# Split activations that begin two columns later: 320-column matmul operands on 16 bytes

## The chip, the cores and the metric

The kernel runs on one core of a Trainium2 chip. The metric is the device time of one execution in microseconds (us); runs before and after are compared by their medians. Single executions are given by the span between the first and last instruction that the profiler saw, and by the time of the whole execution, which is a little longer.

## The reference, cut to what matters

A trunk of two layers over 640 tokens (128 context tokens, 512 latent tokens) of width 2048. Each layer normalizes and modulates its input, multiplies it with a wide input projection, runs two mixers and a gate on parts of the result, and multiplies with an output projection:

```python
shift, scale, gate = modulation(c, ada_w[l], ada_b[l])
h = rms_norm(x, norm_g[l]) * (1.0 + scale[:, None]) + shift[:, None]
...
y, _ = even_mixer(h, w_in_even[e], ...)   # h @ w_in, attention, gated linear attention, gate
...
x = x + gate[:, None] * (y @ w_out[l])
```

Nearly all arithmetic is in `h @ w_in` and `y @ w_out`. The two shifts (one for context, one for latent tokens) are added after the projection: the kernel multiplies them with the same weights as two more columns.

## The kernel before, in words

**Layout.** Activations are stored transposed: a tile has 128 partitions (one block of 128 features) and the tokens lie along the row. There are 16 feature blocks, k = 0 to 15. fp32 accuracy comes from splitting: an activation x becomes `h` (x rounded to the format that TensorE multiplies fast, fp32r) and `l` (x − h), a weight becomes `whi` and `wlo`. One product of a 128x128 weight block and a piece of activations is three matmuls: whi·h, whi·l, wlo·h (`mm_k`, `three`).

**The four tiles.** `acth` and `actl` (`self.ah`, `self.al`, lines 275 and 276) hold the split activations, 16 rows per partition of 2 + 640 words each: two columns for the shifts, then 640 tokens. So a row has 642 words or 2,568 bytes, and the next row begins 8 bytes off a multiple of 16. `eh` and `el` (line 2418 on) hold split combinations of activations for a Strassen-like scheme (`spair`), 6 × 3 rows of `CW` = 2 + 320 words (1,288 bytes). In the compiled program each of the four tiles begins on a multiple of 16 bytes.

**The halves.** A matmul takes at most 512 columns, so the tokens are taken in two halves. `cols` (line 748) gives the columns of each: half 0 is columns 0 to 322 for a projection that needs the shifts (322 wide) and 2 to 322 for one that does not (320 wide); half 1 is columns 322 to 642 (320 wide). In the last pair (`hpair`) the cut is at 384 tokens, so its operands are 384 and 256 wide.

**Who issues matmuls.** `units`, for one output chunk of 128 features: for each four k, half 0 of the four, then half 1 of the four, three matmuls each. `kpair`, for two chunks at the ends of a projection: k by k, both halves at once, the second chunk two steps behind the first. `spair`, for two chunks by seven products instead of eight: `product` runs over the six rows of one combination, `plain` over four k that take no part in it (`JT` and `MT` name the k that are combined).

**Who writes the rows.** `act_mod` (line 1258 on) at the start; `handover` between projections: `rewrite` splits a new activation (ScalarE writes `h`, VectorE or GpSimd writes `l`), `fold` makes the rows of `eh` and `el` and rewrites half 1 of some rows of `acth` and `actl`, after saving them to DRAM (the DMA to `bh_dram` and `bl_dram`). `shifts` and `shift1` write the two shift columns.

**The rest.** `sums` is a work buffer of 322 words. The arena is one region cut by hand into slots of 640 words; its last part, `rest`, holds the slot R, and also the buffers for squares of the outputs (`sqs`, two of 320 words in turn, and `sq`, 384 words for the last pair), which are summed for the norm. All instructions are in an order that a planner in Python (`Pace`) writes out by hand: it keeps a time for each engine and for each block of 32 words of a tile, and its choices (which task to advance, which bank to take) follow from these times.

Of the kernel before, what the change touches and what calls it, by code (L numbers as in the profile page):

```python
# [9 lines left out]
F32 = mybir.dt.float32  # L10
F32R = mybir.dt.float32r
# [3 lines left out]
ALU = mybir.AluOpType  # L15
# [4 lines left out]
KT = D // 128  # L20
NCTX = 128
NLAT = 512
T = NCTX + NLAT
HT = T // 2
# [9 lines left out]
NS = len(JT)  # L34
SUB = NS // 2
NY = 8
CW = 2 + HT
RING = 2560

OUT0 = (0, 12, 1, 13, 2, 14, 3, 15, 8, 10, 9, 11, 4, 5, 6, 7)  # L40
# [200 lines left out]
class Trunk:  # L241
# [9 lines left out]
    def __init__(self, tc, d, es):  # L251
        self.tc, self.d, self.es = tc, d, es
        self.pace = Pace()
        self.nc = Core(self.pace, tc.nc)
        self.n = 0
        self.now = 0.0
        self.turn = {}
        self.tasks = []
        self.low = None
        self.stall = 0.0  # L260
        self.flags = set()
        self.actset = None
        self.folded = self.quiet = False
        self.cut = HT
        self.room = self.rooms[0]
        nc = self.nc
        self.per = es.enter_context(tc.tile_pool(name="per", bufs=1))
        self.sml = es.enter_context(tc.tile_pool(name="sml", bufs=6))
        self.wraws = self.P([128, 2048], "wraw")
        self.whl = [self.P([128, RING], n, F32R) for n in ("whi", "wlo")]  # L270
        ps = es.enter_context(tc.tile_pool(name="ps", bufs=1, space=PSUM))
        self.banks = [ps.tile([128, 512], F32, tag=f"bank{i}", name=f"bank{i}") for i in range(8)]
        self.npj, self.top, self.held, self.nsm = 4, 8, set(), 0

        self.ah = self.P([128, KT, 2 + T], "acth", F32R)
        self.al = self.P([128, KT, 2 + T], "actl", F32R)
        self.Y = self.P([128, NY, T], "Y")
        self.rstd = self.P([128, T], "rstd")
        self.adas = self.P([128, 4 * PIECE + PIECE // 2], "adas")

        self.cT = self.P([128, KT, 2], "cT")
        nc.sync.dma_start(self.cT, d["cT"])
        small = self.P([128, sum(w for _, w in SMALL)], "small")
        nc.scalar.dma_start(small, d["small"])
        at, c = 0, {}
        for name, w in SMALL:
            c[name] = small[:, at : at + w]
            at += w
        self.sel = c["sel"]
        self.adab = c["ada_bT"].rearrange("p (a b) -> p a b", b=48)  # L290
        self.ng = c["norm_gT"].rearrange("p (a b) -> p a b", b=KT)
        self.fg = c["final_gT"]
        self.bg_g = c["gla_bgT"].rearrange("p (a b) -> p a b", b=4)
        self.gn, self.mg, self.m1 = c["gla_gT"], c["gmlp_gT"], c["gla_m1"]
        self.mu = c["gla_mu"].bitcast(U32)
        self.sink = c["attn_sink"]
        self.act(self.cT, self.cT, AF.Silu)
        self.ident = self.P([128, 128], "ident")
        make_identity(tc.nc, self.ident)
        self.ones = self.P([128, 128], "ones")  # L300
        nc.gpsimd.memset(self.ones, 1.0)
        self.eps = self.P([128, 1], "eps")
        nc.gpsimd.memset(self.eps, 1e-6)


        self.b1 = self.P([128, 2, 16], "b1")
        nc.gpsimd.tensor_scalar(self.b1, self.adab[:, :, 16:32], 1.0, None, ALU.add)
        self.A = [self.P([128, KT, 2], f"A{l}") for l in range(2)]
        self.G = [self.P([128, KT, 2], f"G{l}") for l in range(2)]
        self.uses = {}  # L310
        self.yb_pool = tc.tile_pool(name="yb", bufs=1)
        yb = self.yb_pool.__enter__()
        self.YB = self.t(yb, [128, KT - NY, T], "YB")
        self.mixrow = [self.t(yb, [128, PIECE], "mixrow", bufs=2) for _ in range(2)]
        self.prods = [self.t(yb, [128, PIECE], "prod", bufs=2) for _ in range(2)]
        self.made, self.nprod = [], 0
        self.psum = self.P([128, 4, 32], "psum")
        self.part = {k: self.P([128, n, 2], "part" + k) for k, n in (("b0", FIRST), ("g0", 16), ("1", 32), ("g1", 16))}
        for x in self.part.values():
            nc.gpsimd.memset(x, 0.0)  # L320
# [426 lines left out]

    def cols(self, half, shift):
        if half == 0:
            return slice(0 if shift else 2, 2 + self.cut)  # L750
        return slice(2 + self.cut, 2 + T)

    def mm_k(self, c, k, outs, first=0, last=KT - 1, r=0):

# [119 lines left out]
    def spair(self, c1, c2):  # L874
# [8 lines left out]
            if self.chunks[c][3]:  # L883
                self.chunks[c][3]()
        shift = self.chunks[c1][2]
        o = 0 if shift else 2
        full = lambda b: b[:, 0 : CW - o]
        half = lambda b: b[:, 2 - o : CW - o]
        x1 = lambda k: (self.ah[:, k, o:CW], self.al[:, k, o:CW])
        x2 = lambda k: (self.ah[:, k, CW:], self.al[:, k, CW:])  # L890
        tt = lambda f: lambda i: (self.eh[:, i, f, o:CW], self.el[:, i, f, o:CW])
# [106 lines left out]
    def handover(self, ready, free, used, order, at, src, loads, spare, cs, shift=None):  # L998
# [27 lines left out]
        def rewrite():  # L1026
            if shift is not None:
                yield from self.wait("shift1")
            for k in order:
                yield from self.wait(f"{free}:{k}", f"in:{k}", *(f"evac{c}" for c in cs if k in (6, 7)))  # L1030
                x = tile_(k)
                yield from self.until(x)
                while (w := self.pace.ready("a", [self.pace.span(x)], []) - self.now) > 0:
                    yield w
                yield from self.calm(self.calms[0], "ag")
                if shift is not None:
                    for c, a, b in ((0, 0, NCTX), (1, NCTX, T)):
                        y, A, due = x[:, a:b], self.A[1][:, k, c : c + 1], self.pace.t
                        if due["v"] < due["a"]:
                            nc.vector.tensor_scalar(y, y, A, None, ALU.mult)  # L1040
                        else:
                            nc.scalar.activation(y, y, AF.Copy, scale=A)
                h = self.ah[:, k, 2:]
                nc.scalar.activation(h, x, AF.Copy)
                eng = nc.vector if k in self.dve else nc.gpsimd
                eng.tensor_tensor(self.al[:, k, 2:], x, h.bitcast(F32), ALU.subtract)
                self.flags.add(f"{ready}:{k}")
                release(k)
                yield
# [17 lines left out]
        def fold(w):  # L1067
            sub = lambda o, x, y: nc.vector.tensor_tensor(o, x, y, ALU.subtract)
            p = None
            for i in range(w, NS, 2):  # L1070
# [11 lines left out]
                x, y = tile_(j), tile_(m)  # L1082
                sub(q, x[:, two], x[:, one])
                for f in range(3):
                    yield from split(self.eh[:, i, f, 2:CW], self.el[:, i, f, 2:CW], q)
                    if f < 2:
                        sub(q, y[:, one if f else two], q)
                release(j)
# [165 lines left out]
    def act_mod(self, l, k, x, t0, t1):  # L1254

        nc = self.nc
        A = self.A[l]
        for c, a, b in ((0, t0, min(t1, NCTX)), (1, max(t0, NCTX), t1)):
            if a >= b:
                continue  # L1260
            h = self.ah[:, k, 2 + a : 2 + b]
            nc.scalar.activation(h, x[:, a:b], AF.Copy, scale=A[:, k, c : c + 1])
            nc.vector.scalar_tensor_tensor(
                self.al[:, k, 2 + a : 2 + b], x[:, a:b], A[:, k, c : c + 1], h.bitcast(F32), ALU.mult, ALU.subtract
            )


# [107 lines left out]
    def start(self):  # L1375
# [5 lines left out]
        with tc.tile_pool(name="su", bufs=1) as su:  # L1381
# [72 lines left out]
            def shifts():  # L1454
# [51 lines left out]
                    x = self.sh0[:, c, 0:NB]  # L1506
                    nc.vector.tensor_tensor(x, x, self.adab[:, 0, 0:NB], ALU.add)
                yield from self.wait("tiles")
                self.shifts(self.ah[:, :, 0:2], self.al[:, :, 0:2], self.sh0.rearrange("p c f -> p f c"))
                self.flags.add("shift0")  # L1510

                x = self.sh0.rearrange("p c f -> p (c f)")
# [11 lines left out]
            def ready(c, *ks):  # L1524
                return (
                    all((c, k - k % 4, 0) in self.parts for k in ks)
                    and all(f"act{k}" in self.flags for k in ks)
                    and self.left(*self.parts[c, ks[0] - ks[0] % 4, 0], *(a[:, k, 2:] for k in ks for a in (self.ah, self.al))) <= 0.0
                )

            def window(c, k0, n, half):
# [664 lines left out]
    def program(self):  # L2196
# [213 lines left out]
        def open_g0():  # L2410
# [6 lines left out]
            ext = self.es.enter_context(tc.tile_pool(name="ext", bufs=1))  # L2417
            self.eh, self.el = (self.t(ext, [128, NS, 3, CW], n, F32R) for n in ("eh", "el"))
            self.rs = self.t(ext, [128, 4 * NS * 128], "rs")
            self.sums = self.t(ext, [128, CW], "sums")  # L2420
            self.arena(6.17)
            self.slots = {f"Y{i}": Y[:, i, :] for i in range(NY)}
            for n in "ABCDE":
                self.slots[n] = self.take()
# [4 lines left out]
            S = self.slots  # L2429
            L["gz"] = self.xr = Ring([S["A"], S["B"]])  # L2430
            L["ms"] = [S["A"][:, :CUT], S["B"][:, :CUT]]
            self.ssq, self.sq, self.sqs = S["C"], rest[:, 364 : 364 + CUT], Ring([rest[:, 0:HT], rest[:, 364 : 364 + HT]])
            x = self.ar[:, 4 * T : 4 * T + 1024]
            self.wsT, self.gb = (x[:, 512 * i : 512 * i + 512].rearrange("p (a b) -> p a b", b=128) for i in range(2))
            L["vr"] = Ring([S[n] for n in "ABCD"])
# [23 lines left out]
        def shift1():  # L2459
# [1 line left out]
            x = self.part["1"][:, 0:16, :]  # L2461
            self.fin_shift(1, x)
            yield
            self.shifts(self.ah[:, :, 0:2], self.al[:, :, 0:2], x)
            u = self.s("fsh", 12).rearrange("p (a b) -> p a b", b=2)
            for a, b in ((0, 2), (2, NS)):
                j = x[:, JT[a] : JT[a] + b - a, :]
                h, l = (e[:, a:b, :, 0:2] for e in (self.eh, self.el))
                nc.vector.tensor_tensor(u[:, a:b, :], x[:, MT[a] : MT[a] + b - a, :], j, ALU.subtract)
                for f, v, scale in ((0, j, -1.0), (1, j, 1.0), (2, u[:, a:b, :], 1.0)):  # L2470
                    self.split2(h[:, :, f, :], l[:, :, f, :], v, scale)
# [415 lines left out]
```

## Time and profile before

| | us |
|---|---|
| median of 3 runs | 2092.56 |
| lowest and highest | 2092.16, 2093.63 |
| the profiled execution, whole | 2092.06 |
| its span | 2090.3 |
| TensorE matmul busy in the span | 2049.1 |
| VectorE, ScalarE, GpSimd busy | 1324.9, 1065.2, 1275.5 |

In the rows below, PE is a TensorE matmul and PEld a weight load; DVE is VectorE, ACT ScalarE, POOL GpSimd, SP the queue that issues DMAs. `bank<-acth,whi 128*128 128x320` is a matmul that writes a PSUM bank from the moving operand acth (128 partitions, 320 columns) and the weights whi. Matmuls overlap in the array, so a row's duration (some 310 ns) is longer than the distance to the next start (some 147 ns). In a timeline the columns are start, duration, what, and how many were merged into the row; groups give a count, the busy time, the mean duration, and the idle time before them.

### The profile page before, as it was taken

What the parts mean: (1) busy time and instruction counts of PE and PEld (TensorE: products, weight loads), DVE (VectorE), ACT (ScalarE), POOL (GpSimd) and SP (SyncE); (2) the same over time, 40 slices, a digit from 0 to 9 for tenths busy, and PEclk for the clock granted to TensorE, in tenths of its full rate; (3) what the DMA queues carried; (4) which work ended last, traced back from release to release, by engine and by line L of the source; (5) the groups of instructions that cost most, each with busy time, mean ns of one, the idle gap of its engine ahead of it and who ended that gap; (6) DMA issues with size and microseconds to landing.
All of it is one profiled execution on the core that took longest, in us unless ns stands there. A gap on an engine that the chain in (4) does not pass through costs nothing.

```text
span 2090.3 us, 40200 instructions
## 1 busy us (share of the span) xinstructions
PE 2049.1 (98%) x14345; PEld 1998.8 (96%) x14345; DVE 1324.9 (63%) x3070; ACT 1065.2 (51%) x2446; POOL 1275.5 (61%) x1072
## 2 busy tenths in 40 slices
PE   7999999999999999999999999999999999999997
PEld 6889999999999999999999999999999999999997
DVE  4857677676555654798676878787454444456434
ACT  5545555445665765444564434444444544454443
POOL 4655454445555544698665656555655577767984
PEclk9999999999999999999999999999999999999999
DMA  9966433436456445476734455444323344363427
GB/s 367 394 203 199 127 121 110 142 112 191 154 174 190 145 128 164 153 239 224 263 121 119 135 164 157 137 146 149 97 76 95 101 139 132 111 236 109 142 89 252
DMA packets 192698, 340.18 MB, mean 163 GB/s; under 512 B 20753, under 2 KB 70001, under 8 KB 192497
## 3 DMA queue, kind: packets, MB, share of 16 engines
q1 hardware_dynamic: 191296, 336.45, 49.7%
q8 instruction: 112, 1.84, 0.3%
q10 hardware_dynamic: 1200, 1.17, 0.2%
q14 instruction: 90, 0.73, 0.1%
HBM read 303.03 MB, written 31.88 MB: 160 GB/s over the span
## 4 chain that ended last, share of the span: by engine, by line
PE 86%; DMA 5%; DVE 4%; ACT 2%; issue 2%; POOL 1%; SPq 0%; DVEq 0%; POOLq 0%; ACTq 0%
PE bank L399 83%; PE bank L404 2%; DVE Y L214 1%; DVE adas L214 1%; DMA more<-ada 1%; DMA raw<-ada_s 1%; DVE arena L214 1%; DMA Y<-xT 1%; ACT arena L214 1%; DMA Y<-ada 1%; POOL wlo L214 1%; DMA raw<-crow_b 0%; PE bank L1431 0%; DMA adas<-ada 0%; DMA wraw<-w_even 0%
## 5 line engine op out<-in xcount | busy, mean ns | idle before, releaser
L399 PE MATMUL bank<-acth,whi 128*128 128x320 f32 (+3 forms) x3320 | 1018.8, 318 | 4.0 <-DVE YB L214 1.9
L399 PE MATMUL bank<-acth,wlo 128*128 128x320 f32 (+3 forms) x3320 | 992.6, 310 | 0.2
L399 PE MATMUL bank<-actl,whi 128*128 128x320 f32 (+3 forms) x3320 | 992.2, 310 | 0.0
L214 POOL TENSOR_TENSOR wlo<-wraw,whi 128x512 fp32r<-128x512 f32 (+1 forms) x446 | 568.3, 1286 | 434.4 <-ACT whi L214 348.7
L399 PEld LDWEIGHTS bank<-acth,whi 128*128 128x128 f32 (+1 forms) x3320 | 616.2, 188 | 11.6 <-issue 2.6
L399 PEld LDWEIGHTS bank<-actl,whi 128*128 128x128 f32 (+1 forms) x3320 | 616.4, 188 | 1.7
L399 PEld LDWEIGHTS bank<-acth,wlo 128*128 128x128 f32 (+1 forms) x3320 | 616.5, 188 | 0.8 <-POOL wlo L214 0.8
L214 POOL TENSOR_TENSOR wlo<-rs,whi 128x384 fp32r<-128x384 f32 x370 | 411.4, 1130 | 209.0 <-ACT whi L214 162.5
L214 ACT ACTIVATE whi<-wraw 128x512 fp32r<-128x512 f32 (+1 forms) x456 | 261.2, 588 | 130.3 <-PE bank L399 87.9
L214 ACT ACTIVATE whi<-rs 128x384 fp32r<-128x384 f32 x370 | 184.6, 518 | 85.9 <-PE bank L399 69.7
L399 PE MATMUL bank<-eh,whi 128*128 128x322 f32 (+1 forms) x666 | 209.5, 315 | 1.0 <-ACT whi L214 1.0
L399 PE MATMUL bank<-eh,wlo 128*128 128x322 f32 (+1 forms) x666 | 207.0, 311 | 1.0 <-POOL wlo L214 1.0
L399 PE MATMUL bank<-el,whi 128*128 128x322 f32 (+1 forms) x666 | 207.3, 311 | 0.0
L214 DVE CUSTOM_DVE_ANT_0 adas<-adas,bank,partg 128x256 bf16<-128x256 f32 (+1 forms) x296 | 160.7, 543 | 15.0 <-DMA adas<-ada_g 7.4
L214 DVE TENSOR_TENSOR wraw<-rs 128x768 f32<-128x768 f32 x74 | 98.8, 1335 | 100.0 <-DMA rs<-w_odd 49.9
L214 POOL TENSOR_TENSOR prod<-adas,mixrow 128x512 f32<-128x512 f32 x76 | 99.6, 1320 | 67.5 <-ACT prod L214 45.7
L214 ACT ACTIVATE arena<-arena,bc 128x512 f32<-128x512 f32 (+4 forms) x189 | 97.8, 538 | 78.9 <-DVE arena L214 73.9
L399 PEld LDWEIGHTS bank<-eh,wlo 128*128 128x128 f32 x666 | 126.0, 189 | 1.6 <-POOL wlo L214 1.5
L399 PEld LDWEIGHTS bank<-eh,whi 128*128 128x128 f32 x666 | 125.9, 189 | 1.3 <-ACT whi L214 1.2
L214 DVE TENSOR_TENSOR bank<-bank,sums 128x320 f32<-128x320 f32 (+1 forms) x148 | 71.0, 494 | 87.5 <-PE bank L399 65.3
L399 PEld LDWEIGHTS bank<-el,whi 128*128 128x128 f32 x666 | 126.2, 190 | 0.0
L214 DVE CUSTOM_DVE_ANT_0 adas<-adas,bank,part 128x512 bf16<-128x512 f32 x150 | 111.6, 744 | 16.2 <-ACT whi L214 7.1
(226 smaller groups left out, 2450.2 us busy)
## 6 DMA issues: line engine op xcount, KB each, us to landing
wraw<-w_even SPq DMA_DIRECT2D x176, 256.0 KB, 3.4
adas<-ada_g SPq DMA_DIRECT2D x128, 256.0 KB, 3.6
adas<-ada SPq DMA_DIRECT2D x128, 256.0 KB, 3.8
rs<-w_odd SPq DMA_DIRECT2D x50, 384.0 KB, 3.2
wraw<-w_odd SPq DMA_DIRECT2D x74, 256.0 KB, 3.7
wraw<-w_out SPq DMA_DIRECT2D x60, 256.0 KB, 3.6
rs<-w_odd SPq DMA_DIRECT2D x50, 256.0 KB, 3.7
Y<-ada SPq DMA_DIRECT2D x24, 512.0 KB, 7.9
```

What stands on the lines that cost most here:

```text
L214: return f(*args, **kw)
L399: self.nc.tensor.matmul(out, lhsT, rhs, start=start, stop=stop, **kw)
L404: self.nc.tensor.transpose(out, in_, self.ident[:k, :k])
```

## The change

Rows of acth and actl become 4 + 640 words, of eh and el 4 + 320 words. Two unused words come first, then the two shift columns, then the tokens. All slices follow. The work buffer `sums` keeps its size; the arena loses 44 words and the second squares buffer moves up to the end of the first.

```diff
-CW = 2 + HT
+OFF = 4
+CW = OFF + HT
...
-        self.ah = self.P([128, KT, 2 + T], "acth", F32R)
-        self.al = self.P([128, KT, 2 + T], "actl", F32R)
+        self.ah = self.P([128, KT, OFF + T], "acth", F32R)
+        self.al = self.P([128, KT, OFF + T], "actl", F32R)
...
         if half == 0:
-            return slice(0 if shift else 2, 2 + self.cut)
-        return slice(2 + self.cut, 2 + T)
+            return slice(OFF - 2 if shift else OFF, OFF + self.cut)
+        return slice(OFF + self.cut, OFF + T)
...
-        o = 0 if shift else 2
+        o = OFF - 2 if shift else OFF
         full = lambda b: b[:, 0 : CW - o]
-        half = lambda b: b[:, 2 - o : CW - o]
+        half = lambda b: b[:, OFF - o : CW - o]
...
-                h = self.ah[:, k, 2:]
+                h = self.ah[:, k, OFF:]
...
-                    yield from split(self.eh[:, i, f, 2:CW], self.el[:, i, f, 2:CW], q)
+                    yield from split(self.eh[:, i, f, OFF:CW], self.el[:, i, f, OFF:CW], q)
...
-            h = self.ah[:, k, 2 + a : 2 + b]
+            h = self.ah[:, k, OFF + a : OFF + b]
...
-            self.sums = self.t(ext, [128, CW], "sums")
-            self.arena(6.17)
+            self.sums = self.t(ext, [128, 2 + HT], "sums")
+            self.arena(6.1)
...
-            self.ssq, self.sq, self.sqs = S["C"], rest[:, 364 : 364 + CUT], Ring([rest[:, 0:HT], rest[:, 364 : 364 + HT]])
+            self.ssq, self.sq, self.sqs = S["C"], rest[:, HT : HT + CUT], Ring([rest[:, 0:HT], rest[:, HT:T]])
...
-            self.shifts(self.ah[:, :, 0:2], self.al[:, :, 0:2], x)
+            self.shifts(self.ah[:, :, OFF - 2 : OFF], self.al[:, :, OFF - 2 : OFF], x)
...
-                h, l = (e[:, a:b, :, 0:2] for e in (self.eh, self.el))
+                h, l = (e[:, a:b, :, OFF - 2 : OFF] for e in (self.eh, self.el))
```

The three edits left out replace 2 by OFF in the same way (`act_mod`'s write of `l`, `rewrite`'s of `l`, and the first layer's shift columns and readiness check).

More of the change, by code (lines that the diff above doesn't have):

```diff
@@ L1042, in rewrite @@
                             nc.scalar.activation(y, y, AF.Copy, scale=A)
-                h = self.ah[:, k, 2:]
+                h = self.ah[:, k, OFF:]
                 nc.scalar.activation(h, x, AF.Copy)
                 eng = nc.vector if k in self.dve else nc.gpsimd
-                eng.tensor_tensor(self.al[:, k, 2:], x, h.bitcast(F32), ALU.subtract)
+                eng.tensor_tensor(self.al[:, k, OFF:], x, h.bitcast(F32), ALU.subtract)
                 self.flags.add(f"{ready}:{k}")
@@ L1260, in act_mod @@
                 continue
-            h = self.ah[:, k, 2 + a : 2 + b]
+            h = self.ah[:, k, OFF + a : OFF + b]
             nc.scalar.activation(h, x[:, a:b], AF.Copy, scale=A[:, k, c : c + 1])
             nc.vector.scalar_tensor_tensor(
-                self.al[:, k, 2 + a : 2 + b], x[:, a:b], A[:, k, c : c + 1], h.bitcast(F32), ALU.mult, ALU.subtract
+                self.al[:, k, OFF + a : OFF + b], x[:, a:b], A[:, k, c : c + 1], h.bitcast(F32), ALU.mult, ALU.subtract
             )
@@ L1508, in shifts @@
                 yield from self.wait("tiles")
-                self.shifts(self.ah[:, :, 0:2], self.al[:, :, 0:2], self.sh0.rearrange("p c f -> p f c"))
+                self.shifts(self.ah[:, :, OFF - 2 : OFF], self.al[:, :, OFF - 2 : OFF], self.sh0.rearrange("p c f -> p f c"))
                 self.flags.add("shift0")
@@ L1527, in ready @@
                     and all(f"act{k}" in self.flags for k in ks)
-                    and self.left(*self.parts[c, ks[0] - ks[0] % 4, 0], *(a[:, k, 2:] for k in ks for a in (self.ah, self.al))) <= 0.0
+                    and self.left(*self.parts[c, ks[0] - ks[0] % 4, 0], *(a[:, k, OFF:] for k in ks for a in (self.ah, self.al))) <= 0.0
                 )
```

## The prediction

> **What bounds the kernel now.** I read the page first: busy shares, the slices, the chain that ended last.
>
> ```profile
> span 2090.3 us, 40200 instructions
> PE 2049.1 (98%) x14345; PEld 1998.8 (96%) x14345; DVE 1324.9 (63%) x3070; ACT 1065.2 (51%) x2446; POOL 1275.5 (61%) x1072
> ...
> PE   7999999999999999999999999999999999999997
> ...
> PEclk9999999999999999999999999999999999999999
> ...
> PE 86%; DMA 5%; DVE 4%; ACT 2%; issue 2%; POOL 1%; SPq 0%; DVEq 0%; POOLq 0%; ACTq 0%
> ```
>
> TensorE is busy from the second slice to the last but one, at full granted clock, and the chain is 86% TensorE. Only the two ends leave it idle. The split into stretches puts numbers on the first end:
>
> ```profile
> 0.00:105.00 105.00, 89.67 (x1107) 78.23 (x1107) 65.77 (x114) 55.59 (x125) 61.86 (x58) 1.00 1.01 381
> ```
>
> In those 105 us the DMA engines are full (share 1.01) and TensorE waits; after it, a nanosecond saved on a matmul is a nanosecond of the run. So the question is what one matmul costs, and how many there are. The groups by shape, TensorE alone, give the kinds that the change touches:
>
> ```profile
> L399 PE MATMUL bank<-acth,whi 128*128 128x320 f32 x2020 | 622.8, 316 | 4.0 <-DVE YB L214 1.9 <-ACT YB L214 1.4 <-ACT eh L214 0.2
> ...
> L399 PE MATMUL bank<-acth,whi 128*128 128x322 f32 x1204 | 386.4, 321 | 0.0
> ...
> L399 PE MATMUL bank<-eh,whi 128*128 128x322 f32 x450 | 142.2, 316 | 0.0
> ...
> L399 PE MATMUL bank<-eh,whi 128*128 128x320 f32 x216 | 67.3, 311 | 1.0 <-ACT whi L214 1.0
> ```
>
> Each stands for three (hi·hi, lo·hi, hi·lo). Their 316 ns overlap, so they are not the price: that is the **gap**, from one matmul's start to the next one's, about 147 ns.
>
> **A measurement that is already in the trace.** Rows of acth, actl, eh and el are now 642 or 322 words long, so they start on 16 bytes when the row number is even (k; for eh and el 3i+f) and 8 bytes past when it is odd. An operand from column 2 or 322 lies 8 past on even rows and on 16 bytes on odd ones; the 322-wide one from column 0 the reverse. The matmuls' order is fixed by the code, so each row of the timeline has its k. In an output-projection pair (kpair, all 320 wide) twelve matmuls of even rows alternate with twelve of odd rows; the first row of each dozen:
>
> ```profile
> 842.01 0.46 PE L399 MATMUL bank<-acth,whi 128*128 128x320 f32 x2
> ...
> 843.80 0.46 PE L399 MATMUL bank<-acth,whi 128*128 128x320 f32 x2
> ...
> 845.57 0.45 PE L399 MATMUL bank<-acth,whi 128*128 128x320 f32 x2
> ...
> 847.34 0.46 PE L399 MATMUL bank<-acth,whi 128*128 128x320 f32 x2
> ...
> 849.11 0.46 PE L399 MATMUL bank<-acth,whi 128*128 128x320 f32 x2
> ...
> 850.91 0.45 PE L399 MATMUL bank<-acth,whi 128*128 128x320 f32 x2
> ...
> 852.66 0.45 PE L399 MATMUL bank<-acth,whi 128*128 128x320 f32 x2
> ...
> 854.42 0.46 PE L399 MATMUL bank<-acth,whi 128*128 128x320 f32 x2
> ...
> 856.19 0.46 PE L399 MATMUL bank<-acth,whi 128*128 128x320 f32 x2
> ```
>
> Even dozens take 1.79, 1.77, 1.80 and 1.76: 7.12 us for 48, 148.3 ns each. Odd ones 1.77, 1.77, 1.75 and 1.77: 7.06 us, 147.1 ns. An operand 8 bytes off costs here about 1.2 ns more.
>
> Over the whole trace I averaged the gaps after each kind, where the next matmul is one of these kinds too (start times to the nanosecond; of 11,814 such gaps the 426 over 165 ns, waits and restarts behind other kinds of matmul, are left out). First and last row of each kind; even and odd rows are half of it each:
>
> ```profile
> 13.30 0.64 PE L399 MATMUL bank<-acth,suhi 128*128 128x320 f32 x1
> ...
> 2043.76 0.32 PE L399 MATMUL bank<-acth,wlo 128*128 128x320 f32 x1
> ...
> 145.37 0.39 PE L399 MATMUL bank<-acth,whi 128*96 128x322 f32 x1
> ...
> 1862.91 0.31 PE L399 MATMUL bank<-acth,wlo 128*128 128x322 f32 x1
> ...
> 877.37 0.31 PE L399 MATMUL bank<-eh,whi 128*128 128x320 f32 x1
> ...
> 2046.42 0.31 PE L399 MATMUL bank<-eh,wlo 128*128 128x320 f32 x1
> ...
> 1122.84 0.31 PE L399 MATMUL bank<-eh,whi 128*128 128x322 f32 x1
> ...
> 1834.61 0.31 PE L399 MATMUL bank<-eh,wlo 128*128 128x322 f32 x1
> ```
>
> - acth/actl, 320 wide: 6,252 matmuls; even rows (8 past) 147.54 ns, odd rows (on 16) 146.37
> - acth/actl, 322 wide: 3,660; even rows (on 16) 148.20, odd rows (8 past) 148.91
> - eh/el, 320 wide: 648; even 147.73, odd 147.16
> - eh/el, 322 wide: 1,350; even 147.51, odd 147.95
>
> The sign turns with the width, on the same rows, so it goes with the address and not with the place in the loop.
>
> **The change part by part.**
>
> *Operands.* The new pitch is 644 words (eh, el 324), a multiple of 16 bytes, so every row starts alike: 320-wide operands at column 4 or 324, on 16 bytes; 322-wide ones at column 2, 8 bytes past. That is what odd rows have today. **After the change every row lies as an odd row does now**, so the price is half of each kind times (odd − even):
> - 3,126 × (146.37 − 147.54) = −3.67 us
> - 1,830 × (148.91 − 148.20) = +1.29 us
> - 324 × (147.16 − 147.73) = −0.18 us
> - 675 × (147.95 − 147.51) = +0.30 us
>
> Together −2.26 us. The 384- and 256-wide operands of the last pair (192 matmuls in all) I take at −0.1 us, from the 320s' 1.17 ns times the even half. Of the 6,252, 361 run in the first 105 us, where the DMAs set the pace: 361/6,252 × 3.67 = 0.2 us is lost. Sum: −2.2 us.
>
> The other bounds, from gaps between neighbours that lie alike (these matmuls lie among the rows quoted): 320 after 320 both on 16 bytes 146.04 ns (2,249 of them), both 8 past 147.52 (2,106); 322 both on 16 148.07 (1,418), both 8 past 149.15 (1,550). Setting each neighbouring pair of today to its new kind by these means gives −5.8 us for pairs that start 320 wide or lead from 320 to 322, and +3.6 for the rest: −2.2 again. I keep −5.8 (the 322s lose nothing) and +0.7 (322s lose 3.6, 320s gain their least, 0.83 ns between isolated triples, 2.9) as ends.
>
> The Trainium skill speaks against any effect: "TensorE: Matmul & The Clock Gate", section "Wait — 56ns, not 53.3ns?", gives a start-to-start of N ÷ 2.4 GHz + 2.5 ns, whatever the address; by it 320 columns are 135.8 ns and the sum would be 0. The trace disagrees: 146.4 and 147.5 ns by address.
>
> *Writers of these rows* (rewrite, split, act_mod on ScalarE, VectorE, GpSimd) and the saves to DRAM keep count and size:
>
> ```profile
> L214 ACT ACTIVATE acth<-Y x28: 719/738/746, 837.4 to 1881.0; 128x640 fp32r<-128x640 f32 x28
> L435 SPq DMA_DIRECT2D bh_dram<-acth x18: 319/441/589, 853.4 to 1878.1; - x18
> L214 DVE TENSOR_TENSOR el<-bank,eh x54: 474/480/494, 823.5 to 1885.2; 128x320 fp32r<-128x320 f32 x54
> ```
>
> These rows hold both parities already, and their spread bounds the address: 27 ns of 738, 20 of 480. All writers together stay under 3 us on engines idle 37 to 49% of the span, beneath TensorE's queue of matmuls: 0, and if that cover were gone ±1 us. SP's issues keep their place in the queue; the transfers only move their start by 8 bytes at most.
>
> *Squares' buffer.* It moves from word 364 to 320 of its region, right behind the first one.
>
> ```profile
> L214 POOL TENSOR_TENSOR arena<-arena x26: 863/884/1602, 894.5 to 1028.3; 128x320 f32<-128x320 f32 x26
> ```
>
> Two buffers still alternate, they still do not overlap each other, and both lay over the slot R before. No wait is added or removed; the longest of these 26, 1.6 us, is off the chain. 0. The smaller arena loses 44 words that nobody uses.
>
> *Order.* The planner marks time in blocks of 32 words, so a shifted row can flip one of its choices at an edge. What one flip could be worth is bounded by today's longest waits of matmuls:
>
> ```profile
> PE bank L1431 <- DMA Y<-ada: 7.1, 4, 5.3
> ...
> PE bank L399 <- ACT adas L214: 4.5, 4, 2.7
> ```
>
> 2.7 us either way for the projections. I take 0, since whole rows are written at once and their halves keep the same blocks but for the edges.
>
> **The sum:** the profiled execution took 2092.06 us (1.8 us around its span); 2092.06 − 2.2 = 2089.9. The three timed runs' median is 2092.56, 0.5 higher, and the forecast is made for such a median: **2090.4 us**, 0.1% less. A measurement tells about 0.2% (4.2 us) from no change.
>
> **The rivals.**
>
> *The 322s pay nothing* (chance 0.17). Counting pieces of 16 bytes that an operand touches: 1,280 bytes on 16 touch 80, 8 past 81; 1,288 bytes touch 81 either way. Then only the saving stays: −3.67 − 0.18 − 0.1 + 0.2 = −3.8, 2088.8 us; up to −5.8, 2086.8 us. For it: 320s at 147.54 and 146.37 are near 81/80 of one another. Against it: 148.20 against 148.91 for 322s. "SBUF — State Buffer", section "Specifications (TRN2)" of the Trainium skill, says that lines are 16 bytes and each crossing to a new one pays; by that rule this rival is the result.
>
> *No effect* (0.13). The even/odd difference belongs to something that the change keeps, such as the place of k in a weight block (k mod 4), or what is saved returns as waits on POOL's wlo. For it: POOL splits every weight. Against: the reversed sign at 322, and POOL is busy 61%. It gives 2092.6 us.
>
> *322s become much dearer* (0.06). Once all 322s lie 8 past, each may cost the worst that they show today: the last eh triple of 17 S2 products takes 450 ns, 150.0 each.
>
> ```profile
> 1127.70 0.31 PE L399 MATMUL bank<-eh,whi 128*128 128x322 f32 x1
> ...
> 1128.15 0.31 PE L399 MATMUL bank<-acth,whi 128*128 128x320 f32 x1
> ```
>
> The 322s' mean is 148.3 now: 5,010 × 1.7 = +8.5 us, less 3.8: +4.7, 2097.3 us. It decides above 1.6 ns more for each of the 5,010 ((4.2 + 3.8) / 5,010). Against it: those 17 lie on 16 bytes, and odd rows mostly show 148.9.
>
> *A flipped order* (0.04), ±2.7 us: 2087.7 or 2093.1 us, either sign.
>
> **How the numbers follow.** The forecast has 0.60: 2088.9 to 2091.9. The range, **2087.2 to 2093.4**, takes in most of the first rival, all of the second and the upper bound (+0.7); it leaves out the dear 322s and the end of the first rival. Faster by over 0.2% (below 2088.4): half of the first rival, 0.08, some tail of the forecast, 0.06, a lucky order, 0.01: **0.15**. Slower (over 2096.7): the third rival and a little more, **0.06**. Within: **0.79**.
>
> **What would show it.** In the changed kernel's timeline, the dozens of an output-projection pair all take about 1.76 us, with no alternation; 320-wide gaps fall to about 146.3, even rows like odd; 322-wide gaps rise to about 148.7. If 322s stay at 148.0 the first rival holds; if the alternation stays, the second. The number and order of matmuls and waits should not change. It would be wrong if the gaps hang on finer address bits than 16 bytes, or if neighbours that all lie alike run at another pace than today's mixed ones.

## The result, and the profile after

| | before | after |
|---|---|---|
| median, runs | 2092.36 us, 22 runs | 2088.77 us, 22 runs |
| lowest to highest | 2089.26 to 2095.22 | 2085.93 to 2095.23 |
| ratio after to before | | 0.9986 (95%: 0.9979 to 0.9992) |

The changed kernel is 0.14% faster by the ratio, some 3 us (the two medians are 3.6 us apart), and the interval leaves out 1. Two further measurements of it, on other occasions, gave 0.9997 (0.9988 to 1.0006), which does not leave out 1, and 0.9983 (0.9974 to 0.9992), which does.

The program is the same but for addresses: each engine's list of operations, tiles and shapes, in order, is that of before. The page of the execution that was profiled first, its waits of TensorE, and the same groups of twelve matmuls in the output-projection pair that the prediction showed (first row of each dozen, even and odd rows in turn):

```profile
span 2093.0 us, 40200 instructions
...
PE 2047.3 (98%) x14345; PEld 1995.9 (95%) x14345; DVE 1327.3 (63%) x3070; ACT 1064.4 (51%) x2446; POOL 1275.1 (61%) x1072
```

```profile
PE bank L400 <- DVE arena L215: 4.0, 5, 2.2
```

```profile
846.13 0.46 PE L400 MATMUL bank<-acth,whi 128*128 128x320 f32 x2
...
847.90 0.46 PE L400 MATMUL bank<-acth,whi 128*128 128x320 f32 x2
...
849.66 0.45 PE L400 MATMUL bank<-acth,whi 128*128 128x320 f32 x2
...
851.45 0.46 PE L400 MATMUL bank<-acth,whi 128*128 128x320 f32 x2
...
853.21 0.46 PE L400 MATMUL bank<-acth,whi 128*128 128x320 f32 x2
...
854.97 0.46 PE L400 MATMUL bank<-acth,whi 128*128 128x320 f32 x2
...
856.73 0.46 PE L400 MATMUL bank<-acth,whi 128*128 128x320 f32 x2
...
858.49 0.45 PE L400 MATMUL bank<-acth,whi 128*128 128x320 f32 x2
...
860.24 0.45 PE L400 MATMUL bank<-acth,whi 128*128 128x320 f32 x2
```

Two warnings in reading these. The span is longer than before's 2090.3 us although the median is shorter: this execution took 2094.82 us, 6 us over its kernel's median, with one wait of 2.2 us among others. Single executions of one program differ by several us; the gaps between matmuls do not, as experiment e1 shows, so the gaps are the better instrument. And the dozens: even rows now take 1.77, 1.79, 1.76 and 1.76 us (147.5 ns a matmul), odd ones 1.76, 1.76, 1.76 and 1.75 (146.5). Both became faster, but the alternation that the prediction wanted to see vanish is still there, 1.0 ns of 1.2.

The mean gap over the whole trace, by kind as in the prediction (first and last row of the two large kinds):

```profile
13.32 0.64 PE L400 MATMUL bank<-acth,suhi 128*128 128x320 f32 x1
...
2046.48 0.31 PE L400 MATMUL bank<-acth,wlo 128*128 128x320 f32 x1
...
146.52 0.39 PE L400 MATMUL bank<-acth,whi 128*96 128x322 f32 x1
...
1867.63 0.31 PE L400 MATMUL bank<-acth,wlo 128*128 128x322 f32 x1
```

| ns | acth/actl 320 wide | 322 wide | eh/el 320 wide | 322 wide |
|---|---|---|---|---|
| matmuls | 6,252 | 3,660 | 648 | 1,350 |
| before (mean of even and odd rows) | 146.95 | 148.56 | 147.44 | 147.73 |
| forecast for after | 146.37 | 148.91 | 147.16 | 147.95 |
| after | 146.74 | 148.31 | 146.61 | 147.90 |
| change × count | −1.3 us | −0.9 us | −0.5 us | +0.2 us |

The sum, −2.5 us, is near the forecast −2.2. Its parts are not: the large kind gained a third of what was forecast, and the 322s of acth and actl, which should have lost 1.3 us, gained 0.9. Two errors cancelled, so that the sum came near is luck. Split by rows, the 320s of acth and actl now cost 147.00 ns on even rows and 146.48 on odd ones, against 147.54 and 146.37 before: the even rows gained 0.54 of the 1.17 that was forecast, and the odd rows, which already lay on 16 bytes, lost 0.11. The experiments ask why.

### The profile page after: what moved, and what is told of

It is laid out like the page before. It is cut to its first block, busy times and chain, and to the rows that moved or that the text cites. A ratio compares the mean times of both kernels' runs of the same rounds, so it can differ in the third digit from the quotient of the medians.

```text
span 2093.0 us, 40200 instructions
## 1 busy us (share of the span) xinstructions
PE 2047.3 (98%) x14345; PEld 1995.9 (95%) x14345; DVE 1327.3 (63%) x3070; ACT 1064.4 (51%) x2446; POOL 1275.1 (61%) x1072
## 3 DMA queue, kind: packets, MB, share of 16 engines
q10 hardware_dynamic: 1200, 1.17, 0.2%
```

## The experiments

All layouts are variants of the changed kernel: OFF is the token column, the shifts stand in the two columns before it, and the row lengths of acth/actl and of eh/el are made free (`PA`, `PE`). All keep the order of the matmuls; e3, e4 and e8 add a few instructions on GpSimd that clear the unused columns. Two gaps in a row, unless said otherwise, are those of acth and actl, 320 wide and 322 wide. "Sum" below is (mean gap of all kinds − 147.33 ns of before) × 11,814 gaps.

**e1: the changed kernel again.** No edit.

> The changed kernel once more, unchanged, as the yardstick of the gap means (start of a matmul to the start of the next; gaps over 165 ns left out). Its first profile gave 146.74 ns for the 320-wide operands of acth and actl (all on 16 bytes), 148.31 for the 322-wide ones (all 8 past), 146.61 and 147.90 for eh and el. If the gaps are set by addresses, they come out again within 0.1 ns, whatever the whole execution does. If they wander with the execution by 0.3 ns or more, the comparison of profiles says little, and only the times count. Time against the kernel before: 0.998 to 0.999.

Measured: 146.72 and 148.29 ns, eh and el 146.64 and 147.90; sum −2.7 us; ratio 0.9997 (0.9988 to 1.0006). The gaps come out within 0.03 ns of the first profile's while this execution was 6 us shorter than the first profiled one (2088.64 against 2094.82). They belong to the program. The ratio missed the 0.998 to 0.999 expected: the time alone could not have told the change from nothing here.

**e2: all 320s 8 past, all 322s on 16.**

```diff
-OFF = 4
+OFF = 2
+PA, PE = 644, 324
...
-        self.ah = self.P([128, KT, OFF + T], "acth", F32R)
+        self.ah = self.P([128, KT, PA], "acth", F32R)
```

> The same pitch as in the changed kernel (644 and 324 words), but the shift columns at column 0 and the tokens at column 2 again: every 320-wide operand lies 8 bytes past, every 322-wide one on 16. Theory A (the place within 16 bytes sets the gap, by the even and odd rows of before): gaps 147.5 ns (320 wide) and 148.2 (322 wide) for acth and actl, sum +2.3 us against before, ratio 1.001, 4.5 us slower than the changed kernel. Theory B (only the 320s pay, the 322s nothing): 147.5 and 148.5, +3.8 us, ratio 1.002. Theory C (the place within 16 bytes matters little; pitch and finer address bits set it): gaps as in the changed kernel, 146.7 and 148.3, ratio 0.998 to 0.9995.

Measured: 148.79 (320 wide) and 148.21 (322 wide); ratio 1.0034 (1.0022 to 1.0047), 2099.02 against 2092.5 us. Slower than every theory said. Seven dozens of the output-projection pair, the first row of the first one and the row after the last, in e2 and in the changed kernel (e12's profile):

```profile
845.21 0.46 PE L401 MATMUL bank<-acth,whi 128*128 128x320 f32 x2
...
857.72 0.31 PE L401 MATMUL bank<-acth,whi 128*128 128x320 f32 x1
```

```profile
842.91 0.46 PE L400 MATMUL bank<-acth,whi 128*128 128x320 f32 x2
...
855.25 0.31 PE L400 MATMUL bank<-acth,whi 128*128 128x320 f32 x1
```

12.51 us for 84 matmuls, 148.9 ns each, against 12.34, 146.9. So the place within 16 bytes does matter to the 320s, by 2.1 ns in the mean, not by the 1.2 of before's mixed rows: theory C is out. The 322s of acth and actl gain next to nothing on 16 bytes (148.21 against 148.29): for them theory B is nearer. In eh and el the 320s lose 1.3 ns (147.92 against 146.64), and the 322s, now on 16 bytes, lose 0.3 as well (148.21 against 147.90).

**e3: all on 16, and e4: all 8 past.**

```diff
# e3 (OFF = 4)
-            return slice(OFF - 2 if shift else OFF, OFF + self.cut)
+            return slice(0, 0 + 2 + self.cut) if shift else slice(OFF, OFF + self.cut)
# e4 (OFF = 2)
+            return slice(2, 2 + 2 + self.cut) if shift else slice(OFF, OFF + self.cut)
```

The slices in `spair` follow, and the unused columns are set to zero once.

> The changed kernel, but the 322-wide operands begin at column 0 instead of 2, so they lie on 16 bytes too (they then read the unused columns, the shifts and all but two of the tokens, so two tokens of each first half are left out; widths, counts and order stay). Theory A: 146.4 ns (320 wide) and 148.2 (322 wide), sum -5.4 us against before, ratio 0.9974. Theory B: 146.4 and 148.5, -3.8 us, 0.998, the same as the changed kernel. Theory C: no relation; between 0.998 and 1.000.

> The layout of e2, but the 322-wide operands begin at column 2, 8 bytes past, like the 320-wide ones (the shifts are left out and two columns of the other half are read; widths, counts and order stay). Theory A: 147.5 ns (320 wide) and 148.9 (322 wide), sum +5.4 us against before, ratio 1.0026. Theory B: 147.5 and 148.5, +3.8 us, 1.0018. Theory C: no relation; about the same as e2 and the changed kernel, 0.998 to 1.000.

Measured: e3 146.67 and 148.02, sum −3.6 us, ratio 0.9976 (0.9967 to 0.9985). e4 148.86 and 148.17, sum +11.0 us, ratio 1.0039 (1.0025 to 1.0052). With e1 and e2 this is a table of two by two:

| 320 wide / 322 wide, ns | 322s on 16 | 322s 8 past |
|---|---|---|
| 320s on 16 | 146.67 / 148.02 (e3) | 146.72 / 148.29 (e1) |
| 320s 8 past | 148.79 / 148.21 (e2) | 148.86 / 148.17 (e4) |

In these uniform layouts (every row of a tile lies alike) each width has its own price, wherever the other width lies: 2.1 ns for a 320 of acth or actl that is 8 past, 0.3 or nothing for a 322. eh and el show a smaller price for the 320s, 1.3 ns (146.6 and 147.9), and the opposite one for the 322s: 148.2 on 16, 147.9 8 past. So the tile, or its finer address bits, counts too. The forecast's +0.7 for the 322s is not there. e4's sum is twice theory A's.

**e5: alternating rows at another pitch.**

```diff
+OFF = 2
+PA, PE = 646, 326
```

> Tokens at column 2 as before, rows of 646 and 326 words instead of 642 and 322: even and odd rows alternate between 8 past and on 16 bytes as before, but every other address bit is another. Before: 320 wide of acth and actl 147.5 ns (even rows) and 146.4 (odd rows), mean 146.95; 322 wide mean 148.56. The uniform layouts gave 148.8 (8 past) and 146.7 (on 16), whose mean is 147.75. Theory M (alternating itself makes the 8-past rows cheaper, some slack carries over from row to row): 320 wide 146.95 in the mean again, 322 wide 148.5. Theory F (finer address bits made before's pitch cheap): the 320s' mean is another one, near 147.75, and the 322s' near 148.2.

Measured: 320 wide 147.98 on rows 8 past and 146.38 on rows on 16, mean 147.18; 322 wide 148.40; one time, 2096.69 against 2094.21 us of before. Neither theory alone. Rows 8 past are cheaper between rows on 16 (147.5 at pitch 642, 148.0 here) than among their like (148.8); that much is theory M. But 0.2 ns in the 320s' mean and 0.8 in those of eh and el (148.20 against 147.44) go with the pitch, which is theory F. Of the two mixed pitches tried, 642 words was the better.

The traces tell the two apart further, if the same matmuls are compared from run to run by their place in the order. In before and in e5, most rows 8 past come in runs of three matmuls between rows on 16 (`units`), and some in runs of twelve (`kpair`):

| 320-wide matmuls of acth and actl that before has 8 past, ns | before (642) | e5 (646) | e2 (all 8 past) | e4 (all 8 past) |
|---|---|---|---|---|
| 2,404 in runs of three | 147.29 | 147.74 | 148.47 | 148.59 |
| 242 in runs of twelve | 148.43 | 148.97 | 148.83 | 148.85 |

In runs of twelve a mixed layout costs what a uniform one does within 0.4 ns; in runs of three it is 0.7 to 1.3 ns cheaper, at both pitches. So the cheapness of mixed rows belongs to short runs, and the pitch adds some 0.5 ns to either.

**e6: 648 words.**

```diff
+PA, PE = 648, 328
```

> Everything placed as in the changed kernel (320 wide on 16 bytes, 322 wide 8 past), rows of 648 and 328 words. Theory P (the gap is the number of 16-byte pieces that the operand touches, 80 or 81): 146.7 ns (320 wide) and 148.3 (322 wide) again, within 0.2. Theory F (finer bits): another pitch gives other means, 0.5 ns or more apart.

Measured: 146.99 and 147.95, eh and el 147.16 and 148.31; one time, 2091.49 against 2094.21 us. That is 0.3 to 0.5 ns to either side of the changed kernel: another pitch, with the place within 16 bytes kept, moves a kind by some tenths, and the sum by 1.3 us (−1.4 instead of −2.7).

**e7: tokens at column 3.**

```diff
-OFF = 4
+OFF = 3
+PA, PE = 644, 324
```

> The changed kernel with the tokens at column 3 instead of 4 and the shifts at column 1: 320-wide operands lie 12 bytes past, 322-wide ones 4 past. Theory P: both touch 81 pieces of 16 bytes, so 148.8 ns and 148.2, as with everything 8 past (148.86 and 148.17), some 8 us over the kernel before. If an odd number of words costs more than 8 bytes do, the gaps are over 149.

Measured: 320 wide **145.67**, 322 wide 148.19; eh and el 145.41 and 149.08; one time, 2086.74 against 2094.21 us. Theory P falls: 12 past, a 320-wide operand touches 81 pieces of 16 bytes and is faster than with 80. The 322s of eh and el, now 4 past, pay 1.2 ns more than 8 past.

**e8: 324 wide instead of 322.**

```diff
-            return slice(OFF - 2 if shift else OFF, OFF + self.cut)
+            return slice(0 if shift else OFF, OFF + self.cut)
```

> The changed kernel, but the 322-wide operands are 324 wide and begin at column 0, on 16 bytes (two unused columns are multiplied too, and the sums come out two columns further right than they are read; order and counts stay). Theory P: 324 columns on 16 bytes touch 81 pieces, as 322 do, so 148.2 ns as before, nothing gained or lost against 322 wide. Theory N (the gap goes by columns; between 256 and 320 wide it grew by 0.44 ns a column): 149.1 ns.

Measured: 148.50 (acth, actl) and 148.64 (eh, el), against 148.29 and 147.90 for 322 wide: 0.2 and 0.7 ns more; but the place changed with the width. Beside e3, where the 322s lie on 16 bytes too (148.02, and 148.18 for eh and el), two more columns cost 0.5 ns in both pairs of tiles: about half of theory N's 0.9, and not theory P's nothing.

**e9: column 3 again, timed; e10: column 3 at 648 words; e11: column 5 at 648 words; e12: the changed kernel a third time.**

```diff
+OFF = 3            # e9: PA, PE = 644, 324; e10: PA, PE = 648, 328
+OFF = 5            # e11: PA, PE = 648, 328
```

> The layout of e7 (tokens at column 3, 12 bytes past; shifts at column 1) once more, now timed. Theory P is out: this place touches 81 pieces and had the lowest gaps, 145.67 ns (320 wide). If the gaps are set by addresses they come out again within 0.1 ns. By the gap means of all kinds (147.33 ns before, 146.58 here, some 11,800 matmuls) it is 8.9 us faster than the kernel before, ratio 0.9958; if the single time of e7 was luck and the gaps don't carry over into the time, 0.998 or above.

> Tokens 12 bytes past and shifts 4 past as in e7, rows of 648 and 328 words. Theory Q (the place within 16 bytes has its own price: 0 gives 146.7, 8 gives 148.8, 12 gives 145.7): 145.7 ns again within 0.3 (320 wide of acth and actl). Theory F (12 bytes past only happened to fit the pitch of 644): 146.5 or more.

> Tokens at column 5, shifts at column 3, rows of 648 and 328 words: 320-wide operands lie 4 bytes past, 322-wide ones 12 past. Open. If an odd number of words is what helps, 4 past is as good as 12: 145.7 ns. If the price follows the pieces of 16 bytes and 12 past is the exception, 148 or more. For the 322-wide ones 12 past gives 146.7 to 147 if that place helps them as it helps the 320s, 148.2 if nothing in their place matters.

> The changed kernel on the same chip as e9, for a third time. Gap mean 147.10 ns against 147.33 before over some 11,800 matmuls: 2.7 us faster, ratio 0.9987. The two measurements so far are 0.9986 (0.9979 to 0.9992) and 0.9997 (0.9988 to 1.0006). If the time holds what the gaps give, this one lies between 0.998 and 0.9995; if the gain is lost elsewhere, at 1.000.

| | 320 wide, ns | 322 wide, ns | sum, us | time |
|---|---|---|---|---|
| e9, 12 past / 4 past | 145.67 | 148.16 | −9.0 | 0.9962 (0.9949 to 0.9974), 2084.92 us |
| e10, the same at 648 | 145.78 | 148.46 | −7.7 | 2085.28 us, one run |
| e11, 4 past / 12 past | 149.41 | 147.34 | +11.7 | 2100.69 us, one run |
| e12, on 16 / 8 past | 146.73 | 148.28 | −2.8 | 0.9983 (0.9974 to 0.9992), 2088.58 us |

The kernel before had 2092.8 us beside these. The same seven dozens in e9 and in e11:

```profile
840.83 0.45 PE L401 MATMUL bank<-acth,whi 128*128 128x320 f32 x2
...
853.08 0.31 PE L401 MATMUL bank<-acth,whi 128*128 128x320 f32 x1
```

```profile
846.50 0.46 PE L401 MATMUL bank<-acth,whi 128*128 128x320 f32 x2
...
859.11 0.32 PE L401 MATMUL bank<-acth,whi 128*128 128x320 f32 x1
```

12.25 us and 12.61 us for 84 matmuls, 145.8 and 150.1 ns; between them lie e12's 146.9 and e2's 148.9. 12 past keeps its price at another pitch (145.67, 145.78), so theory Q holds: the place within 16 bytes has a price. For 320 columns of acth and actl it is 145.7 to 145.8 (12 past), 146.7 to 147.0 (on 16), 148.8 (8 past, one pitch) and 149.4 (4 past, one pitch); in eh and el the order is the same, 145.4 to 145.6, 146.6 to 147.2, 147.9 and 150.0. For 322 columns of acth and actl it is 147.3 (12 past, one pitch) and else 147.9 to 148.5; in eh and el 147.0 (12 past) and else 147.9 to 149.1, dearest 4 past at pitch 324. An odd number of words is neither good nor bad in itself.

A stretch with 320-wide operands alone shows it without averaging: from 1876 to 2030 us the kernel runs the last output projection. The rows count the matmuls of the one line in it (stretch, its length, TensorE's busy time, count, granted clock, DMA share, GB/s). Before, e2, e12, e9:

```profile
1876.00:2030.00 154.00, 153.28 (x1039) 1.00 0.38 122
```

```profile
1876.00:2030.00 154.00, 153.90 (x1035) 1.00 0.39 128
```

```profile
1876.00:2030.00 154.00, 154.00 (x1052) 1.00 0.38 119
```

```profile
1876.00:2030.00 154.00, 153.94 (x1059) 1.00 0.37 117
```

That is 1,039 matmuls (with 0.7 us of idle time), 1,035, 1,052 and 1,059 in the same time, at full granted clock (1.00 in each row).

e9 beats both kernels: the changed one by 0.2% (2084.92 against 2088.58 us on the same occasion), the one before by 0.4%. Its tokens begin one column after before's, where the change moved them by two.

## Why the prediction was right, and where its working failed

*TensorE bounds the run, and a nanosecond of gap is a nanosecond of time.* Held in sign throughout. The change gained 2.5 to 2.8 us by gaps in its three profiles, and 3.6, 1.4 and 4.2 us by medians; e3 gained 3.6 by gaps and 5.0 by medians, e9 9.0 and 7.9. Losses came out smaller in the time than in the gaps: e2 11.1 us by gaps, 6.5 by medians; e4 11.0 and 7.1. The traces show where part of the rest stayed: the gaps beside other kinds of matmul, waits among them, add up to 285.0, 285.9 and 285.3 us in the dearer layouts e2, e4 and e11, against 288.3 in before's profile and 286.9 to 291.3 in those of the changed kernel, e1, e3, e6 and e9. Why they shrink was not tried.

*The place within 16 bytes changes the gap.* Right, and the largest effect of the study. It was mis-sized: 1.2 ns from mixed rows, 2.1 ns between uniform layouts (1.3 in eh and el).

*"After the change every row lies as an odd row does now", so it costs what an odd row costs now.* This step failed. The place was right, the price was not: even rows came down to 147.00 ns, not to 146.37, and odd rows went up to 146.48. The term −3.67 us for the 320s measured −1.3: 3,126 × (147.00 − 147.54) = −1.7 and 3,126 × (146.48 − 146.37) = +0.3. Two things had been taken for the price of the place. First, rows 8 past cost less in short runs between rows on 16 than among their like (147.29 against 148.47 ns in runs of three, the table at e5). So alternating had hidden much of what the change was to save: 146.95 in the mean, where uniform rows would give (146.7 + 148.8) / 2 = 147.75. Second, even and odd rows can differ though all 320s lie alike: by 0.5 ns in the changed kernel (147.00 and 146.48), by 0.1 in e3 (146.74 and 146.61), and the other way in e2 (148.56 and 149.04). Why a row 8 past is cheaper in a short run, and whether this contrast belongs to finer address bits, to the neighbours or to the row's place in the loop, stays open.

*The 322s lose 1.29 and 0.30 us.* Wrong for acth and actl, −0.9; near for eh and el, +0.2. In uniform layouts of one pitch acth's and actl's 322s cost 148.0 to 148.3, on 16 or 8 past; the 148.91 of before's odd rows, 8 past, became 148.36 in the changed kernel, where the same rows still lie 8 past, so the contrast was one of the mixed layout as well. On this point the first rival was nearly right.

*The first rival's price*, 2088.8 us, came nearest to the median, 2088.77, but not by its own working: it kept −3.67 for the 320s, and its count of pieces fell with e7. The Trainium skill's rule beside it ("SBUF — State Buffer", section "Specifications (TRN2)": lines of 16 bytes, each crossing to a new one pays) agrees with 0 against 8 past (148.8 / 146.7 = 1.014, 81 / 80 = 1.0125) and not with 12 past, which also touches 81 and costs 145.7, nor with 4 past, 81 too and 149.4.

*No effect* is out by the intervals of the first and third measurement and by e2 to e4. In part it was right: of the contrast between even and odd rows, 0.5 of 1.2 ns remained in the whole trace with all rows placed alike, and 1.0 of 1.2 in the pair that the prediction showed, so that stretch was a poor witness for a sound effect.

*Dear 322s* and *a flipped order*: neither happened; 148.3 ns, and the same order on every engine.

*Writers, squares' buffer, arena:* nothing to be seen. e2 to e12 share the moved buffer and the smaller arena, and their times go the way of the matmuls' gaps. An undoing of the buffer alone was not run.

The forecast 2090.4 us is 1.6 over the measured median, 2088.77. That median lies within the whole range of 2087.2 to 2093.4, but just under the forecast's own part of it, 2088.9 to 2091.9. By the ratio the forecast is nearer: 0.9990 against 0.9986, or 2090.4 against 2089.6 for the median of 2092.56 that it was made for.

## What to carry to other kernels

Where TensorE is never idle, the distance between starts of matmuls, averaged by kind over one profile, tells a change of 0.1% that ten timed runs leave open; it came out within 0.03 ns in repeated profiles. A contrast found inside one kernel (even against odd rows) is a price in that mixture: before a layout is made uniform, measure the uniform layout, and compare the same matmuls in both. And try all places of an operand within 16 bytes, not only the round one: here the best for 320 columns was 12 bytes past.

## What the runs showed of the hardware that was not expected

- A 128x320 operand of acth or actl cost 145.7, 146.7, 148.8 or 149.4 ns by its place 12, 0, 8 or 4 bytes past a multiple of 16, and one of eh or el 145.4, 146.6, 147.9 or 150.0. The cause of that order is open.
- A 320-wide operand 8 bytes past cost 147.3 ns in runs of three between operands on 16 bytes, and 148.5 where all its neighbours lay 8 past too.
- "TensorE: Matmul & The Clock Gate" of the Trainium skill, section "Wait — 56ns, not 53.3ns?", gives N ÷ 2.4 GHz + 2.5 ns with no term for the address, an estimate of 135.8 ns for 320 columns; no place here had a mean below 145.4.
- Gaps repeat with the program: the 320s of acth and actl in three profiles of one program, on three occasions, gave 146.74, 146.72 and 146.73 ns.
